# A hybrid pooling and mLSTM layer on one core: where the first phase's transposes, weight casts and modulation stand

## The chip, the core and the metric

The kernel runs on one NeuronCore of a Trainium2 chip. Time is device time in microseconds (us) of one launch, as the median of several runs; lower is better. The engines are named as in the profile: PE (TensorE, matrix products), PEld (PE's weight loads), DVE (VectorE), ACT (ScalarE), POOL (GpSimd) and SP (SyncE, which issues most DMAs).

## What is computed

One layer of a diffusion backbone over 512 latent tokens and 256 context tokens with 1024 channels: modulated RMSNorm, one input projection, a pooling mixer and a bidirectional mLSTM, an output projection, then a modulated RMSNorm and a SwiGLU feed-forward part. Cut to what the change touches:

```python
mod = silu(c) @ w_ada + b_ada              # the same for c_ctx
sh1, sc1, g1, sh2, sc2, g2 = split(mod, 6)
a_lat = rmsnorm(x, norm_mix) * (1 + sc1) + sh1
a_ctx = rmsnorm(ctx, norm_mix) * (1 + csc1) + csh1
p_lat = a_lat @ w_in                       # IN_COLS = 7 * 1024 + 16
p_ctx = a_ctx @ w_in
```

## The kernel before

All products run in float32 on PE with operands that are split in two: `h` is the operand rounded to a shorter format (an ACT cast) and `l` is what is left (a DVE subtraction); a product is then the sum of three, `h*h`, `h*l` and `l*h`. Activations are stored with channels on the 128 partitions, so x is eight blocks (k = 0 to 7) of 128 channels by 512 tokens.

The **first phase** (L352 to L399, about the first 61 us) computes the modulation `sh1, sc1`, the normalised and modulated activations `aT[k]`, and at the same time six column tiles of the input projection (`FIRST`), each accumulated over k in a PSUM bank of its own (`acc0`). Its loop runs over k. The order of PE, ACT and DVE is written out by hand in this phase (`manual_schedule`, L263 to L400): each of these engines takes its instructions in the order in which the code issues them. Behind L400 a scheduler orders them, and it may put instructions of later code between those of the phase. SP's order is the scheduler's too. What belongs to block k:

- `mod_rows(k)` (L272): a DMA of 1 MB of w_ada (`ada`, three buffers), eight small products (L279) into a PSUM bank, and an ACT copy of the result into SBUF (L282).
- `mod_cols(k)` (L285): two PE transposes of that copy (L288) turn rows into columns; three small DVE operations (L290, L292, L293) make from them the shift `shm[k]` and the scale `sm[k]`.
- `stage(k)` (L334): a DMA of six weight tiles (`wr`, three buffers), their cast on ACT (L339, `wh`, two buffers), and through `modulate` (L295) the activation: DVE multiplies x by scale and by the norm's factor (L299), ACT adds the shift and casts (L300, the `h` half `a`), DVE computes the weights' `l` half (L341, `wl`, two buffers), and DVE the activation's `l` half (L303).
- `products(k)` (L344): 18 matmuls (L347), six banks by three halves, in the order `(wh, ah)`, `(wh, al)`, `(wl, ah)` in each bank.

Before the loop, blocks 0 and 1 are staged. The loop's step k issues the first nine products of k, `mod_rows(k + 2)`, the other nine products, then `mod_cols(k + 2)` and `stage(k + 2)`. So block k + 2 is ready one whole step before it is used. Further work hangs on some of the steps: in steps 0 to 3 two squares and their sums for the context's norm (L220 to L227), at the end of step 4 and step 5 the norm's factor of the context (PE products L237 and L253, DVE L243, an ACT copy L395), at the end of steps 5 and 6 `ctx_quad` (L313), which modulates four blocks of the context each (four DVE operations L325, four of ACT L327, four of DVE L329), and in step 6 the load of the weights for the values (L154, L157, L158). After the phase PE goes on to the values' products (L578 to L580).

Two instructions of later code matter below. `crow_setup` (L424) loads the conditioning row `crow_s`, takes its tanh on ACT (L96, into `pb`) and combines the two on DVE (L100). They have no place of their own in the hand-written order.

Of the kernel before, what the change touches and what calls it, by code (L numbers as in the profile page):

```python
# [10 lines left out]
F32 = mybir.dt.float32  # L11
F32R = mybir.dt.float32r
# [7 lines left out]
KT = D // P  # L20
# [30 lines left out]
def layer_kernel(ctx: ExitStack, tc, xT, cT, w0, w1, wv0, wv, wada_a, wada_b, par, crow, bg, wpool,  # L51
                 wout, wffi, wffo, icnt, consts, out):
    nc = tc.nc
    V = nc.vector
# [16 lines left out]
    def tl(tag, shape, dtype=F32, bufs=1, align=None):  # L71
        cnt[0] += 1
        return homes[tag].tile(shape, dtype, name=f"{tag}_{cnt[0]}", tag=tag, bufs=bufs, align_bytes=align)

    def S(tag, dtype=F32):
        return tl(tag, [P, T], dtype, BUFS[tag], HALFLINE if tag in shifted else LINE)
# [4 lines left out]
    def PS(tag="ps"):  # L81
        cnt[0] += 1
        return ps.tile([P, 512], F32, name=f"{tag}{cnt[0]}", tag=tag, bufs=4)
# [7 lines left out]
    def small(shape, nm, dtype=F32, home="small"):  # L91
        return homes[home].tile(shape, dtype, name=nm, tag=nm, bufs=1)
# [13 lines left out]
    def pcol(base, j):  # L106
        return parm[:, base + j:base + j + 1]
# [21 lines left out]
    x_sb = []  # L129
# [69 lines left out]
    def vload(src, n, i):  # L199

        _, wh, wl = wload(src[:, i * 4 * n:(i + 1) * 4 * n], 4 * n, skip=min(NEXT, WMAX - 4 * n))
        return [(wh[:, c * n:(c + 1) * n], wl[:, c * n:(c + 1) * n]) for c in range(4)]
# [63 lines left out]
    rs_x = S("m")  # L266

    mods = small([P, 48], "mods")
    sm = small([P, KT, 2], "sm")
    shm = small([P, KT, 2], "shm")  # L270

    def mod_rows(k):  # L272

        raw = tl("ada", [P, KT, 256], F32, 3)
        nc.sync.dma_start(raw.rearrange("p k c -> p (k c)"), wada_a[k])
        acc = PS()
        for r in range(2):
            for g in range(4):
                nc.tensor.matmul(acc[32 * g:32 * g + 32, :256], sil[:, 4 * r + g, :], raw[:, 4 * r + g, :],  # L279
                                 start=r == 0, stop=r == 1, tile_position=(0, 32 * g))  # L280
        rows = S("tmp")
        nc.scalar.copy(rows[:, :256], acc[:, :256])  # L282
        return rows

    def mod_cols(k, rows):  # L285
        bank = PS()
        for w in range(2):
            nc.tensor.transpose(bank[:, w * P:(w + 1) * P], rows[:, w * P:(w + 1) * P], ident)  # L288
        both = tl("rc2", [P, 2, 2], F32, 2)
        V.tensor_reduce(both, bank[:, :2 * P].rearrange("p (w g j) -> p w j g", w=2, g=4)[:, :, 0:2, :],  # L290
                        mybir.AxisListType.X, ALU.add)
        V.tensor_scalar(shm[:, k, :], both[:, 0, :], pcol(C_BA, k), None, ALU.add)  # L292
        V.tensor_scalar(sm[:, k, :], both[:, 1, :], bsc1[:, k:k + 1], pcol(C_NM, k), ALU.add, ALU.mult)  # L293

    def modulate(src, r, scale, shift, h, l, between=None):  # L295

        t1 = S("tmp")
        t1 = t1[:, :src.shape[-1]]
        V.scalar_tensor_tensor(t1, src, scale, r, ALU.mult, ALU.mult)  # L299
        nc.scalar.activation(h, t1, AF.Identity, bias=shift)  # L300
        if between:
            between()
        V.scalar_tensor_tensor(l, t1, shift, h.bitcast(F32), ALU.add, ALU.subtract)  # L303
        return h, l

    aT, acT = [], []
# [6 lines left out]
    def ctx_quad(k):  # L313

        if k == 0:
            tl("before_ac", [P, NEXT], F32, 1, HALFLINE)
        t, h, l = [], [], []
        for e in range(4):
            if e % 2 == 0:
                tt, hh, ll = S("tmp"), S("ac", F32R), S("ac", F32R)  # L320
            o = e % 2 * TC
            t.append(tt[:, o:o + TC])
            acT.append((hh[:, o:o + TC], ll[:, o:o + TC]))
        for e in range(4):
            V.scalar_tensor_tensor(t[e], c_sb[k + e], sm[:, k + e, 1:2], rs_c[:, :TC], ALU.mult, ALU.mult)  # L325
        for e in range(4):
            nc.scalar.activation(acT[k + e][0], t[e], AF.Identity, bias=shm[:, k + e, 1:2])  # L327
        for e in range(4):
            V.scalar_tensor_tensor(acT[k + e][1], t[e], shm[:, k + e, 1:2], acT[k + e][0].bitcast(F32),  # L329
                                   ALU.add, ALU.subtract)  # L330

    w_first = []

    def stage(k, r):  # L334

        n = len(FIRST) * P
        raw, wh, wl = tl("wr", [P, WMAX], F32, 3), tl("wh", [P, WMAX], F32R, 2, LINE), tl("wl", [P, WMAX], F32R, 2, LINE)
        nc.sync.dma_start(raw[:, :n], w0[k])
        nc.scalar.copy(wh[:, :n], raw[:, :n])  # L339
        aT.append(modulate(x_sb[k], r, sm[:, k, 0:1], shm[:, k, 0:1], S("a", F32R), S("a", F32R),  # L340
                           lambda: V.tensor_sub(wl[:, :n], raw[:, :n], wh[:, :n].bitcast(F32))))  # L341
        w_first.append([(wh[:, i * P:(i + 1) * P], wl[:, i * P:(i + 1) * P]) for i in range(len(FIRST))])

    def products(k, lo, hi, parts=((0, 0), (0, 1), (1, 0))):  # L344
        for i in range(lo, hi):
            for w, x in parts:
                nc.tensor.matmul(acc0[i], w_first[k][i][w], aT[k][x], start=k + w + x == 0, stop=k == KT - 1 and w == 1)  # L347
# [12 lines left out]
    for t, q in enumerate((sq[0], sq[KT - 1])):  # L360
# [3 lines left out]
        if t == 0:  # L364
            keep_warm(WARM[1], warm)
    sd = stx.power(bank, T // P)
    rows = mod_rows(0)
    keep_warm(WARM[2], warm)
    mod_cols(0, rows)
    r = stx.rstd_rows(sd, ALL)  # L370
    stage(0, r)
    keep_warm(WARM[3], warm)
    rows = mod_rows(1)
    keep_warm(WARM[4], warm)
    products(0, 0, nf, ((0, 0),))
    mod_cols(1, rows)
    nc.scalar.copy(rs_x, r)
    stage(1, rs_x)
    for k in range(KT):
        parts = ((0, 0), (0, 1), (1, 0))[0 if k else 1:]  # L380
        products(k, 0, nf // 2, parts)
        if k + 2 < KT:
            rows = mod_rows(k + 2)
        products(k, nf // 2, nf, parts)
        if k + 2 < KT:
            mod_cols(k + 2, rows)
            stage(k + 2, rs_x)
        if k < 4:
            nc.sync.dma_start(cxt[k], cT[:, k * 512:(k + 1) * 512])
            for e in range(2):  # L390
                stc.add(c_sb[2 * k + e], slice(0, TC))
        if k == 4:
            sd = stc.rstd_cols(slice(0, TC))
        if k == 5:
            nc.scalar.copy(rs_c[:, :TC], stc.rstd_rows(sd, slice(0, TC)))  # L395
        if k == KT - 2:
            wv_first = vload(wv0, DH + NG, 0)
        if k in (5, 6):
            ctx_quad(4 * (k - 5))  # L399
# [129 lines left out]
    late = iter(range(16, 48))  # L529
# [596 lines left out]
    r = st1.rstd_rows(sd, HALF[0])  # L1126
# [13 lines left out]
    class Half:  # L1140
# [26 lines left out]
        def low(self):  # L1167
            V.tensor_sub(self.dst[1][:, self.c], self.s[:, self.c], self.dst[0][:, self.c].bitcast(F32))

    with tc.manual_schedule(engines={mybir.EngineType.PE, mybir.EngineType.Activation, mybir.EngineType.DVE}):  # L1170
# [5 lines left out]
        r = st1.rstd_rows(sd, HALF[1])  # L1176
# [233 lines left out]
```

## Time and profile before

| | |
|---|---|
| median of 3 runs | 887.27 us (884.91 to 887.32) |
| the profiled execution's own time | 886.11 us |
| its span, first to last instruction | 884.3 us |
| PE busy | 874.4 us, 99% |
| DVE busy | 614.7 us, 70% |
| ACT busy | 436.7 us, 49% |
| mean granted clock of PE | 0.998 |

The profile is one execution. A row of the timeline reads: start in us, length in us, engine, line of the kernel, operation, what is written and read, shapes, how often, and in brackets the idle time before it and who ended it. Neighbouring matmuls overlap in the rows (a row is longer than the step to the next one), so PE's pace is read from the starts.

### The profile page before, as it was taken

The page shows a single profiled execution, that of the slowest core. Times are in us where ns is not written, and L with a number is a line of the kernel's source. Part 1 is how long each engine was busy: PE and PEld are TensorE (multiplying, and loading weights), DVE is VectorE, ACT ScalarE, POOL GpSimd, SP SyncE. Part 2 cuts the span into 40 slices and gives each one's busy share as a digit, 9 for nine tenths or more (in the row PEclk, how much of TensorE's full clock was granted, in tenths as well). Part 3 has the DMA queues.
Part 4 walks back from the last instruction along what each step waited for, and adds up shares of the span by engine and source line. Part 5 has one row for each costly group of instructions (what it writes and reads, how often), then busy time and mean ns, then how long its engine had stood idle before and what let it go on. Part 6 is the DMA issues. An engine that isn't in the chain of part 4 may idle for free.

```text
span 884.3 us, 15057 instructions
## 1 busy us (share of the span) xinstructions
PE 874.4 (99%) x5920; PEld 797.7 (90%) x5920; DVE 614.7 (70%) x1187; ACT 436.7 (49%) x823; POOL 66.7 (8%) x93
## 2 busy tenths in 40 slices
PE   9999999999999999999999999999999999999997
PEld 7689798899888998889988899999889998899996
DVE  4678677877876787767886767795366753867644
ACT  4464354455344453444455446673255741666542
POOL 0000010020000100000000000120011100111000
PEclk9999999999999999999999999999999999999999
DMA  9863021436252542434454830384366643755502
GB/s 349 324 196 113 25 72 57 164 113 180 72 187 88 170 141 84 155 109 135 142 149 125 294 111 1 104 221 107 95 176 147 145 119 87 206 142 125 144 1 96
DMA packets 41446, 120.88 MB, mean 137 GB/s; under 512 B 4480, under 2 KB 8864, under 8 KB 40352
## 3 DMA queue, kind: packets, MB, share of 16 engines
q1 hardware_dynamic: 35904, 109.96, 38.2%
q0 software_dynamic: 5472, 9.96, 6.8%
q8 instruction: 46, 0.75, 0.3%
q14 instruction: 24, 0.20, 0.1%
HBM read 116.22 MB, written 3.69 MB: 136 GB/s over the span
## 4 chain that ended last, share of the span: by engine, by line
PE 96%; DVE 1%; ACT 1%; DMA 1%; issue 0%; DVEq 0%; SPq 0%; ACTq 0%
PE ps L187 14%; PE ps L189 13%; PE ps L188 13%; PE ps L197 8%; PE ps L195 8%; PE ps L194 8%; PE pat L347 3%; PE ps L578 3%; PE ps L579 3%; PE ps L580 3%; PE pat L187 2%; PE pat L189 2%; PE pat L188 2%; PE pat L792 2%; PE pat L793 2%; PE pat L794 2%
## 5 line engine op out<-in xcount | busy, mean ns | idle before, releaser
L157 ACT CAST wh<-wr 128x1024 fp32r<-128x1024 f32 (+3 forms) x78 | 78.9, 1011 | 102.7 <-PE ps L188 45.6
L158 DVE TENSOR_TENSOR wl<-wr,wh 128x1024 fp32r<-128x1024 f32 (+3 forms) x78 | 92.6, 1188 | 35.9 <-ACT wh L157 23.8
L194 PE MATMUL ps<-a,wh 128*128 128x512 f32 x272 | 106.5, 392 | 0.0
L195 PE MATMUL ps<-a,wh 128*128 128x512 f32 x272 | 106.3, 391 | 0.0
L187 PE MATMUL ps<-act,wh 128*128 128x512 f32 (+1 forms) x199 | 69.2, 348 | 0.0
L188 PE MATMUL ps<-act,wh 128*128 128x512 f32 (+1 forms) x199 | 69.0, 347 | 0.0
L189 PE MATMUL ps<-act,wl 128*128 128x512 f32 (+1 forms) x199 | 69.0, 347 | 0.0
L197 PE MATMUL ps<-a,wl 128*128 128x512 f32 x272 | 68.0, 390 | 0.0
L195 PEld LDWEIGHTS ps<-a,wh 128*128 128x128 f32 x272 | 51.1, 188 | 10.2
L194 PEld LDWEIGHTS ps<-a,wh 128*128 128x128 f32 x272 | 51.1, 188 | 10.2
L197 PEld LDWEIGHTS ps<-a,wl 128*128 128x128 f32 x272 | 50.8, 188 | 10.5
L1030 POOL DMA_DIRECT2D ol<-in_wffi x38 | 33.4, 897 | 254.7 <-ACT ol L1029 124.4
L187 PE MATMUL ps<-hp,gh 128*128 128x256 f32 x176 | 49.9, 284 | 0.4 <-ACT gh L176 0.4
L189 PE MATMUL ps<-hp,ol 128*128 128x256 f32 x176 | 48.8, 277 | 0.5 <-DVE ol L1027 0.5
L188 PE MATMUL ps<-hp,gh 128*128 128x256 f32 x176 | 49.0, 278 | 0.0
L1251 DVE SCALAR_TENSOR_TENSOR x<-ps,lb,x 128x512 f32<-128x512 f32 (+1 forms) x32 | 19.6, 616 | 42.1 <-PE ps L189 42.1
L189 PE MATMUL ps<-hp,gl 128*128 128x256 f32 x176 | 48.9, 278 | 0.0
L187 PE MATMUL ps<-hp,oh 128*128 128x256 f32 x176 | 48.8, 277 | 0.0
L188 PE MATMUL ps<-hp,oh 128*128 128x256 f32 x176 | 48.7, 277 | 0.0
L537 DVE SCALAR_TENSOR_TENSOR pb<-pb,crow_s 128x1024 f32<-128x1024 f32 x32 | 38.9, 1233 | 10.1 <-DMA pb<-in_wada_b 10.1
L187 PEld LDWEIGHTS ps<-act,wh 128*128 128x128 f32 x199 | 37.5, 188 | 4.8
L188 PEld LDWEIGHTS ps<-act,wh 128*128 128x128 f32 x199 | 37.5, 188 | 4.8
(365 smaller groups left out, 2726.4 us busy)
## 6 DMA issues: line engine op xcount, KB each, us to landing
wr<-in_w SPq DMA_DIRECT2D x42, 512.0 KB, 3.5
pb<-in_wada_b SPq DMA_DIRECT2D x32, 512.0 KB, 4.2
wr<-in_wffi SPq DMA_DIRECT2D x25, 512.0 KB, 4.3
ur<-in_wffi SPq DMA_DIRECT2D x19, 512.0 KB, 4.0
ol<-in_wffi POOLq DMA_DIRECT2D x38, 256.0 KB, 4.9
ada<-in_wada_a SPq DMA_DIRECT2D x8, 1024.0 KB, 9.8
wr<-in_wffo SPq DMA_DIRECT2D x16, 448.0 KB, 3.6
wr<-in_wout SPq DMA_DIRECT2D x8, 512.0 KB, 3.5
```

What stands on the lines that cost most here:

```text
L157: nc.scalar.copy(wh, raw[:, :n])
L158: V.tensor_sub(wl, raw[:, :n], wh.bitcast(F32))
L187: nc.tensor.matmul(dst, wh, ah, start=first and i == 0, stop=False, skip_group_check=on)
L188: nc.tensor.matmul(dst, wh, al, start=False, stop=False, skip_group_check=on)
L189: nc.tensor.matmul(dst, wl, ah, start=False, stop=last and i == n - 1, skip_group_check=on)
L194: nc.tensor.matmul(dst, wh, ah, start=first and i == 0, stop=False)
L195: nc.tensor.matmul(dst, wh, al, start=False, stop=False)
L197: nc.tensor.matmul(dst, wl, ah, start=False, stop=last and i == len(wparts) - 1)
L347: nc.tensor.matmul(acc0[i], w_first[k][i][w], aT[k][x], start=k + w + x == 0, stop=k == KT - 1 and w == 1)
L537: V.scalar_tensor_tensor(wa[:, :D], wa[:, :D], 0.5, crow_s, ALU.mult, ALU.mult, accum_out=mods[:, i:i + 1])
L578: nc.tensor.matmul(acc[:, :n], ah, wh, start=kk == 0, stop=False)
L1030: nc.gpsimd.dma_start(l, dram, accum_op=ALU.add)
```

## The change

`stage` is cut in two: `first_weights(k)` (DMA, cast, and the weights' `l` half) and `modulated(k)` (the activation). `mod_rows` can leave its ACT copy to a later call of `mod_copy`. Blocks 0 and 1, staged before the loop, are as before. In the loop:

```diff
-    def stage(k, r):
+    def first_weights(k, sub=True):
...
+    def modulated(k, r, between=None):
+        aT.append(modulate(x_sb[k], r, sm[:, k, 0:1], shm[:, k, 0:1], S("a", F32R), S("a", F32R), between))
+
+    def stage(k, r):
+        modulated(k, r, first_weights(k, False))
...
     for k in range(KT):
         parts = ((0, 0), (0, 1), (1, 0))[0 if k else 1:]
+        ahead = 0 < k < KT - 1
+        if ahead:
+            first_weights(k + 1)
         products(k, 0, nf // 2, parts)
+        if ahead:
+            mod_cols(k + 1, rows)
         if k + 2 < KT:
-            rows = mod_rows(k + 2)
+            acc = mod_rows(k + 2, True)
+        if ahead:
+            modulated(k + 1, rs_x)
+        if k + 2 < KT:
+            rows = mod_copy(acc)
         products(k, nf // 2, nf, parts)
-        if k + 2 < KT:
-            mod_cols(k + 2, rows)
-            stage(k + 2, rs_x)
         if k < 4:
```

The transposes and the modulation of a block thus move from the end of the step two before its use into the middle of the step just before its use. The arithmetic is the same. Lines behind the change are numbered 13 to 19 higher (the products L347 become L360, the transposes L288 become L291, the context's L325, L327 and L329 become L328, L330 and L332).

On PE, in step 3, the rows before show the modulation's products for block 5 between two groups of nine products, and the transposes for the same block at the end of the step (`a` and `wh`, `wl` are the operands of step 3; the last row is the first of step 4):

```order
L347 MATMUL pat_150<-a_367,wl_364 128x512
L279 MATMUL ps_449<-ada_447,sil 32x256 x8
L347 MATMUL pat_151<-a_367,wh_363 128x512
...
L347 MATMUL pat_109<-a_367,wl_364 128x512
L288 MATMUL ps_469<-ident,tmp_458 128x128 x2
L347 MATMUL ps_148<-a_424,wh_420 128x512
```

In the changed kernel the same place on PE reads:

```order
L360 MATMUL pat_150<-a_395,wl_364 128x512
L291 MATMUL ps_434<-ident,tmp_401 128x128 x2
L279 MATMUL ps_443<-ada_441,sil 32x256 x8
L360 MATMUL pat_151<-a_395,wh_363 128x512
...
L360 MATMUL pat_109<-a_395,wl_364 128x512
```

The transposes, now those of block 4, stand directly ahead of the modulation's products, and nothing stands between the last product of a step and the first of the next, except L237 and L253 at the ends of steps 4 and 5.

On DVE, at the end of step 5, the rows before are the last of block 7 (`rc_119` and `a_595`), then the context's `ctx_quad`, then the row of `crow_setup`:

```order
L290 TENSOR_REDUCE rc_119_585<-ps_582 128x4
L292 TENSOR_SCALAR shm<-rc_119_585,parm 128x2
L293 TENSOR_SCALAR sm<-rc_119_585,bsc_89,parm 128x2
L299 SCALAR_TENSOR_TENSOR tmp_596<-x_103,sm,m_144 128x512
L341 TENSOR_TENSOR wl_591<-wr_589,wh_590 128x768
L303 SCALAR_TENSOR_TENSOR a_595<-tmp_596,shm,a_594 128x512
L325 SCALAR_TENSOR_TENSOR tmp_606<-cx_153,sm,m_157 128x256 x2
L325 SCALAR_TENSOR_TENSOR tmp_609<-cx_154,sm,m_157 128x256 x2
L329 SCALAR_TENSOR_TENSOR ac_608<-tmp_606,shm,ac_607 128x256 x2
L329 SCALAR_TENSOR_TENSOR ac_611<-tmp_609,shm,ac_610 128x256 x2
L100 SCALAR_TENSOR_TENSOR crow_s<-pb_706,crow_s 128x1024
```

In the changed kernel the same work on DVE (`a_566` is the last of block 6; `wl_607`, `rc_130` and `a_628` belong to block 7) reads:

```order
L306 SCALAR_TENSOR_TENSOR a_566<-tmp_567,shm,a_565 128x512
L328 SCALAR_TENSOR_TENSOR tmp_587<-cx_153,sm,m_157 128x256 x2
L328 SCALAR_TENSOR_TENSOR tmp_590<-cx_154,sm,m_157 128x256 x2
L332 SCALAR_TENSOR_TENSOR ac_589<-tmp_587,shm,ac_588 128x256 x2
L332 SCALAR_TENSOR_TENSOR ac_592<-tmp_590,shm,ac_591 128x256 x2
L346 TENSOR_TENSOR wl_607<-wr_605,wh_606 128x768
L293 TENSOR_REDUCE rc_130_623<-ps_620 128x4
L100 SCALAR_TENSOR_TENSOR crow_s<-pb_706,crow_s 128x1024
L295 TENSOR_SCALAR shm<-rc_130_623,parm 128x2
L296 TENSOR_SCALAR sm<-rc_130_623,bsc_89,parm 128x2
L302 SCALAR_TENSOR_TENSOR tmp_629<-x_103,sm,m_144 128x512
L306 SCALAR_TENSOR_TENSOR a_628<-tmp_629,shm,a_627 128x512
```

All of block 7 now stands behind the context's eight operations, and the row of `crow_setup` stands inside it. On ACT the same piece before, from the copy of block 7's modulation rows (`tmp_571`) on:

```order
L282 COPY tmp_571<-ps_562 128x256
L339 CAST wh_590<-wr_589 128x768
L96 ACTIVATE pb_706<-crow_s 128x1024
L300 ACTIVATE a_594<-tmp_596,shm 128x512
L395 COPY m_157<-ps_601 128x256
L327 ACTIVATE ac_607<-tmp_606,shm 128x256 x2
L327 ACTIVATE ac_610<-tmp_609,shm 128x256 x2
L157 CAST wh_644<-wr_642 128x1088
```

and in the changed kernel:

```order
L285 COPY tmp_571<-ps_556 128x256
L414 COPY m_157<-ps_582 128x256
L330 ACTIVATE ac_588<-tmp_587,shm 128x256 x2
L330 ACTIVATE ac_591<-tmp_590,shm 128x256 x2
L342 CAST wh_606<-wr_605 128x768
L96 ACTIVATE pb_706<-crow_s 128x1024
L303 ACTIVATE a_627<-tmp_629,shm 128x512
L157 CAST wh_644<-wr_642 128x1088
```

On ACT, too, the cast of block 7's weights and its activation now follow the context's four operations. On SP the context's loads (`cx`) now stand one place ahead of the weights' loads (`wr`) in the first steps, and the load of `crow_s` stands behind the second load for the values (L154) and not ahead of it. POOL's order is the same.

More of the change, by code (lines that the diff above doesn't have):

```diff
@@ L270, in layer_kernel, with mod_rows @@
     shm = small([P, KT, 2], "shm")
-    def mod_rows(k):
+    def mod_rows(k, late=False):
         raw = tl("ada", [P, KT, 256], F32, 3)
@@ L280, in mod_rows, with mod_copy @@
                                  start=r == 0, stop=r == 1, tile_position=(0, 32 * g))
+        return acc if late else mod_copy(acc)
+    def mod_copy(acc):
         rows = S("tmp")
@@ L339, in stage, with low @@
         nc.scalar.copy(wh[:, :n], raw[:, :n])
-        aT.append(modulate(x_sb[k], r, sm[:, k, 0:1], shm[:, k, 0:1], S("a", F32R), S("a", F32R),
-                           lambda: V.tensor_sub(wl[:, :n], raw[:, :n], wh[:, :n].bitcast(F32))))
         w_first.append([(wh[:, i * P:(i + 1) * P], wl[:, i * P:(i + 1) * P]) for i in range(len(FIRST))])
+        def low():
+            V.tensor_sub(wl[:, :n], raw[:, :n], wh[:, :n].bitcast(F32))
+        if sub:
+            low()
+        return low
+    def modulated(k, r, between=None):
+        aT.append(modulate(x_sb[k], r, sm[:, k, 0:1], shm[:, k, 0:1], S("a", F32R), S("a", F32R), between))
+    def stage(k, r):
+        modulated(k, r, first_weights(k, False))
     def products(k, lo, hi, parts=((0, 0), (0, 1), (1, 0))):
```

## The prediction, as it was put on record

> **What bounds the kernel now.** I read the page first, then the waits of PE over the whole run, then the timelines of PE, DVE and ACT for the first 61 us, where the change acts. The page's chain of waits, by engine:
>
> ```profile
> span 884.3 us, 15057 instructions
> PE 96%; DVE 1%; ACT 1%; DMA 1%; issue 0%; DVEq 0%; SPq 0%; ACTq 0%
> ```
>
> The path to the end is PE. The waits of PE in the whole run (line waited for, total us, times, longest):
>
> ```profile
> PE ps L189 <- DVE ol L1027: 0.5, 1, 0.5
> PE pat L752 <- ACT tmp L803: 0.4, 1, 0.4
> PE pat L189 <- DMA ol<-in_wffi: 0.4, 1, 0.4
> PE ps L187 <- ACT gh L176: 0.4, 1, 0.4
> PE pat L666 <- DVE g_nM L664: 0.2, 1, 0.2
> ```
>
> Behind the start PE waits for others 1.9 us in all, none of it in the first phase. PE takes its matmuls in order, so a microsecond that PE loses at 57 us has almost nothing later in which to vanish: at most these 1.9. The change can act in two ways: by what PE itself does in a step, and by making PE wait where it doesn't now.
>
> **What a step costs PE.** Step 2 to step 3 on PE (starts, then lengths; the steps between starts count):
>
> ```profile
> 31.45 0.39 PE L347 MATMUL pat<-a,wl 128*128 128x512 f32 x1
> 31.77 1.07 PE L279 MATMUL ps<-ada,sil 128*32 128x256 f32 x16
> ...
> 34.74 0.40 PE L347 MATMUL pat<-a,wl 128*128 128x512 f32 x1
> 34.98 0.38 PE L288 MATMUL ps<-ident,tmp 128*128 128x128 f32 x2
> 35.12 0.71 PE L347 MATMUL ps<-a,wh 128*128 128x512 f32 x2
> 35.66 0.40 PE L347 MATMUL ps<-a,wl 128*128 128x512 f32 x1
> ```
>
> and the ends of steps 4 and 5, the start of step 7, and the first values' product behind it:
>
> ```profile
> 46.14 0.38 PE L288 MATMUL ps<-ident,tmp 128*128 128x128 f32 x2
> 46.36 0.51 PE L237 MATMUL ps<-ones,tmp 128*128 128x2 f32 x4
> 46.72 0.71 PE L347 MATMUL ps<-a,wh 128*128 128x512 f32 x2
> ...
> 52.18 0.38 PE L288 MATMUL ps<-ident,tmp 128*128 128x128 f32 x2
> 52.40 0.61 PE L253 MATMUL ps<-ident,rc 128*128 128x128 f32 x4
> 52.76 0.71 PE L347 MATMUL ps<-a,wh 128*128 128x512 f32 x2
> ...
> 56.96 0.61 PE L347 MATMUL ps<-a,wh 128*128 128x512 f32 x2
> ...
> 61.04 0.28 PE L578 MATMUL ps<-wh,a 128*128 128x272 f32 x1
> ```
>
> The 18 products of step 7, with nothing between them, take 61.04 - 56.96 = 4.08 us, 0.227 each. Against that pace three borders cost extra. (i) From a product to the modulation's products: 31.77 - 31.45 = 0.32, so 0.09 extra. (ii) From transposes back to products: two products in 35.66 - 35.12 = 0.54 and not 0.455, so 0.09 extra. (iii) From transposes to other small products: 46.36 - 46.14 = 0.22, where transposes ahead of products take 35.12 - 34.98 = 0.14, so 0.08 extra.
>
> **The change on PE.** Each loop step with modulation products had borders (i) and (ii); now it has (iii) in their place. Counted up to the first product of step 6: (ii) falls away four times (starts of steps 1 to 4), (i) five times but comes back twice (products now stand directly ahead of L237 and L253), (iii) comes five times and goes twice, and one pair of transposes, block 7's, has moved behind this point. That is -4 x 0.09 - 3 x 0.09 + 3 x 0.08 - 0.14 = -0.53 us: L253 would start at 52.40 - 0.53 = 51.87 and step 6 at 52.23. The changed order's border is not in the trace at this place; L237's row is the nearest. Ends: only the transposes' 0.14, or 0.8 if (iii) costs nothing. Block 7's transposes come back in step 6 with 0.14 + 0.09, so PE alone would win 0.3 us by step 7, which would start at 56.96 - 0.53 + 0.23 = 56.66.
>
> **The wait in steps 1 to 5.** The modulation chain was a step ahead; now it must end between the middle of a step and its end. Its measured lengths, on DVE for block 5, with ACT's part:
>
> ```profile
> 35.40 0.17 DVE L290 TENSOR_REDUCE rc<-ps 128x4 f32<-128x16 f32 x1 [1.77 <-PE ps L288]
> ...
> 36.06 0.75 DVE L299 SCALAR_TENSOR_TENSOR tmp<-x,sm,m 128x512 f32<-128x512 f32 x1
> 36.73 0.95 DVE L341 TENSOR_TENSOR wl<-wr,wh 128x768 fp32r<-128x768 f32 x1
> 37.61 0.75 DVE L303 SCALAR_TENSOR_TENSOR a<-tmp,shm,a 128x512 fp32r<-128x512 f32 x1
> ```
>
> ```profile
> 34.94 0.83 ACT L339 CAST wh<-wr 128x768 fp32r<-128x768 f32 x1 [1.61 <-PE pat L347]
> 36.85 0.72 ACT L300 ACTIVATE a<-tmp,shm 128x512 fp32r<-128x512 f32 x1 [1.07 <-DVE tmp L299]
> ```
>
> Transposes start at 34.98; reduce +0.42; L299 +0.66; ACT's half +0.79; DVE's half +0.76 and 0.75 long: 3.38 us, plus 0.04 of handover (ACT ends at 37.57, DVE starts at 37.61). PE takes from the transposes to the second product of the next step, the first that reads the `l` half: 0.22, then 34.98 - 31.77 = 3.21 from the modulation's products to the step's end, then 0.23: 3.66 us. It fits with 0.24 to spare. The cast starts where it did, since it waited and waits for PE to free `wh` (the bracket of its row), so cast and subtraction, 0.83 and 0.95, are done before the transposes, 2 us into the step. The context's squares and sums stand behind the chain and ahead of the next cast, covered by the same 2 us. The queue of SP has the context's loads ahead of the weights' now; the weights have a step in hand. I cost these steps' waits at nothing; with the cover gone they cost five times what exceeds 0.24.
>
> **The wait ahead of step 7.** Here the context's block stands in between. Its rows on DVE and ACT:
>
> ```profile
> 55.48 1.67 DVE L325 SCALAR_TENSOR_TENSOR tmp<-cx,sm,m 128x256 f32<-128x256 f32 x4
> 57.07 1.67 DVE L329 SCALAR_TENSOR_TENSOR ac<-tmp,shm,ac 128x256 fp32r<-128x256 f32 x4
> 58.65 1.23 DVE L100 SCALAR_TENSOR_TENSOR crow_s<-pb,crow_s 128x1024 f32<-128x1024 f32 x1
> 59.78 1.30 DVE L158 TENSOR_TENSOR wl<-wr,wh 128x1088 fp32r<-128x1088 f32 x1
> ```
>
> ```profile
> 52.92 1.06 ACT L96 ACTIVATE pb<-crow_s 128x1024 f32<-128x1024 f32 x1
> ...
> 54.68 0.35 ACT L395 COPY m<-ps 128x256 f32<-128x256 f32 x1
> ...
> 56.00 1.72 ACT L327 ACTIVATE ac<-tmp,shm 128x256 fp32r<-128x256 f32 x4 [0.96 <-DVE tmp L325]
> 57.62 1.09 ACT L157 CAST wh<-wr 128x1088 fp32r<-128x1088 f32 x1
> ```
>
> In the order before, block 7 was finished on DVE ahead of L325 (the first row starts at 55.48), and PE needed it at 56.96; the context's eight operations delayed nobody. Now they stand ahead of block 7, and cannot start until L253 has run:
>
> - L253 from 51.87, 0.61 long; copy on ACT 0.35, two handovers of 0.04: DVE's four start at 52.91.
> - Four by 57.07 - 55.48 = 1.59, four by 58.65 - 57.07 = 1.58: DVE free at 56.08. ACT meanwhile starts its four 0.52 later than DVE's, takes 57.62 - 56.00 = 1.62 and then casts block 7's weights in 0.83: done at 55.88, in time.
> - The weights' subtraction, 37.61 - 36.73 = 0.88: 56.96.
> - Reduce to L299 takes 0.66, and `crow_s` between them 59.78 - 58.65 = 1.13: 58.75. Its tanh on ACT (1.06 behind the cast) is ready by 56.95, just in time.
> - ACT's half at +0.79, 59.54; DVE's half at +0.76, 60.30, 0.75 long, handover 0.04: 61.09.
>
> PE's second product of step 7 waits for that; by PE's own pace it would come at 56.66 + 0.23 = 56.89. So PE stands **4.2 us**. The other 16 and itself follow at 17 x 0.227 = 3.86: the values' products start at 64.95 in place of 61.04, **3.9 us later**. The 0.3 us won is in that sum. Queued behind the waiting product on PE is the rest of the kernel. The values' weights (cast on ACT and L158 on DVE, 1.1 and 1.3 us) come behind block 7, while PE still has 3.86 us of step 7: hidden.
>
> Two loads stand behind this. `crow_s` now follows the second values' load:
>
> ```profile
> 48.87 0.33 SPq L154 DMA_DIRECT2D wr<-in_wv  x1
> crow_s<-in_crow SPq DMA_DIRECT2D x1, 512.0 KB, 4.7
> ```
>
> Issued 0.4 us behind that load, or earlier, it lands at 54 at the latest, ahead of its tanh at 55.8.
>
> Bounds: with the gain up to L253 between 0.14 and 0.8 (0.53 taken) the shift is 4.3 or 3.6; a dozen handovers read to 0.05 add 0.4 either way: +3.2 to +4.7.
>
> **Clock while PE stands.** In slices of the first microseconds (PE busy and its count of matmuls after the slice's length; the clock column reads 1.00) PE starts slowly:
>
> ```profile
> 4.00:5.00 1.00, 1.00 (x7) 1.00 (x7) 0.00 (x0) 0.00 (x0) 0.00 (x0) 1.00 1.07 397
> 7.00:8.00 1.00, 1.00 (x11) 1.00 (x10) 0.69 (x1) 0.90 (x3) 0.00 (x0) 1.00 1.02 414
> ```
>
> The same warm-up matmuls come at 7 per us and later at 11, the change lying near 6 us, some 5 us after PE's first. If PE fell back to that pace after its wait, 5 us of it would cost 5 x (1 - 7/11) = 1.8 us. The wait here would be 3.5 us without any matmul, then one product, then 0.6 more. [...] No wait of this length follows the start in this trace, so it cannot show it; by the row alone I leave the sum at 3.9.
>
> **From the profile to the time.** The profiled execution took 886.11 us; plus 3.9 it would take 890.0. It lay 1.2 below the median of the runs; on the median, 887.27 + 3.9 = **891.2 us**.
>
> **Rivals.**
> - Clock: the pace drops after the wait, 887.27 + 5.7 = 893.0. For it: the slow start. [...] 0.14.
> - Tight steps: the chain's 0.24 in steps 1 to 5 is not there, say 0.3 short of it each time: 3.9 + 5 x 0.3, 892.7. Against: every length in it is measured in the same surroundings. 0.07.
> - Lost time comes back: the delay gives DVE, ACT and DMA a lead that removes PE's five later waits, 1.9 us: 889.3. Against: four of the five are fed by PE's own results. 0.08.
> - Other side: block 7 isn't held up, because DVE reaches it ahead of the context's operations; then PE keeps its 0.3, 887.0. It decides at 56.9: the chain must end 4.2 us earlier than I sum it, which is the context's eight operations and `crow_s` together (1.59 + 1.58 + 1.13 = 4.3). The order shows these ahead of it on the same engine. 0.05.
>
> My forecast keeps 0.66. A measurement of this kernel can tell about 0.3%, 2.7 us, from no change: slower means above 889.9. The forecast lies 1.3 above that, with 0.8 of its own bounds and runs that spread by 2.4; I give it 0.86 on that side: 0.57, with the two dearer rivals 0.78. Same: the rest of the forecast and the cheaper rivals, 0.19; faster 0.03. The range leaves out the other side, part of the returned time and the ends of the dearer cases: 888.8 to 893.8.
>
> **What would show it.** In the profile after: L253 near 51.9; L328 directly behind its copy; L346 of block 7 near 56; a wait of PE at L360 for ACT's half and then DVE's half (L303, L306) of 3 to 4 us in all between 56 and 61.5; the values' products (L597) near 65; no other new wait. A wait of PE in steps 1 to 5, or a step 7 whose products come at less than the 0.227 pace, would be the rivals. Wrong I would be if step 7 starts before 58 us.

## The result, and the profile after

| | before | after |
|---|---|---|
| median of 6 runs each, side by side | 886.12 us (884.91 to 887.32) | 892.61 us (891.62 to 893.9) |
| the profiled execution's own time | 886.11 us | 893.9 us |
| its span | 884.3 us | 892.1 us |
| mean granted clock of PE | 0.998 | 0.994 |

The ratio is 1.0077, 95% interval [1.0067, 1.0087]: slower by 6.5 us. The forecast was 891.2, 3.9 us more than before. The time lies in the range, the sign is right, and 2.6 us of the loss are not in the sum. The profiled execution of after is the slowest of its six (7.8 us above before's), so the size of the loss is taken from the medians.

The chain of waits by engine, and the waits of PE (line waited for, total us, times, longest):

```profile
span 892.1 us, 15054 instructions
PE 94%; DVE 3%; DMA 1%; ACT 1%; issue 0%; DVEq 0%; SPq 0%; POOL 0%; POOLq 0%
```

```profile
PE ps L360 <- ACT a L303: 3.5, 2, 3.4
PE pat L143 <- DVE warm L114: 1.4, 1, 1.4
PE ps L187 <- ACT pm L176: 1.0, 1, 1.0
```

The first three rows of the waits are shown. The first is new: the products of the first phase wait for ACT's half of an activation. Twice, but 0.15 us of it lies at 17.72; the 3.4 are one wait. PE's timeline around it, up to the first product of the values:

```profile
56.16 0.39 PE L360 MATMUL pat<-a,wl 128*128 128x512 f32 x1
59.91 1.58 PE L360 MATMUL ps<-a,wh 128*128 128x512 f32 x2 [3.35 <-ACT a L303]
61.29 0.63 PE L360 MATMUL ps<-a,wl 128*128 128x512 f32 x1
61.72 1.05 PE L360 MATMUL ps<-a,wh 128*128 128x512 f32 x2
62.57 0.63 PE L360 MATMUL ps<-a,wl 128*128 128x512 f32 x1
...
66.06 0.39 PE L360 MATMUL pat<-a,wl 128*128 128x512 f32 x1
66.29 0.63 PE L360 MATMUL pat<-a,wh 128*128 128x512 f32 x2
66.75 0.40 PE L360 MATMUL pat<-a,wl 128*128 128x512 f32 x1
66.99 0.29 PE L597 MATMUL ps<-wh,a 128*128 128x272 f32 x1
```

Two things are to be seen. The product that starts at 56.16 is the last one until 59.91: the wait of the prediction. And behind it a group of three products takes 62.57 - 61.29 = 1.28 us, 0.43 each, where the last three take 66.75 - 66.06 = 0.69, 0.23 each: PE runs at half its pace until 65.6. The slices of after say so in their clock column (the number ahead of the last two):

```profile
56.00:59.90 3.90, 0.55 (x3) 0.13 (x1) 3.08 (x7) 1.32 (x3) 0.23 (x3) 0.86 0.45 142
59.90:65.60 5.70, 5.69 (x13) 4.13 (x14) 4.02 (x8) 2.63 (x5) 0.00 (x0) 0.50 0.71 203
65.60:66.90 1.30, 1.30 (x7) 1.08 (x6) 1.30 (x4) 1.11 (x3) 0.00 (x0) 0.98 0.71 204
```

If the clock is either full or half, as the two paces say, 0.86 over 3.9 us means 2 x 0.14 x 3.9 = 1.1 us at half, then 5.7, then 0.05: 6.8 us together.

Why PE waits stands on DVE and ACT:

```profile
52.63 1.68 DVE L328 SCALAR_TENSOR_TENSOR tmp<-cx,sm,m 128x256 f32<-128x256 f32 x4 [1.16 <-ACT m L414]
54.23 1.67 DVE L332 SCALAR_TENSOR_TENSOR ac<-tmp,shm,ac 128x256 fp32r<-128x256 f32 x4
55.81 0.96 DVE L346 TENSOR_TENSOR wl<-wr,wh 128x768 fp32r<-128x768 f32 x1
56.67 0.17 DVE L293 TENSOR_REDUCE rc<-ps 128x4 f32<-128x16 f32 x1
56.76 1.22 DVE L100 SCALAR_TENSOR_TENSOR crow_s<-pb,crow_s 128x1024 f32<-128x1024 f32 x1
...
58.35 0.75 DVE L302 SCALAR_TENSOR_TENSOR tmp<-x,sm,m 128x512 f32<-128x512 f32 x1
59.89 0.75 DVE L306 SCALAR_TENSOR_TENSOR a<-tmp,shm,a 128x512 fp32r<-128x512 f32 x1 [0.79 <-ACT a L303]
```

```profile
54.77 0.82 ACT L342 CAST wh<-wr 128x768 fp32r<-128x768 f32 x1
55.50 1.06 ACT L96 ACTIVATE pb<-crow_s 128x1024 f32<-128x1024 f32 x1
59.13 0.72 ACT L303 ACTIVATE a<-tmp,shm 128x512 fp32r<-128x512 f32 x1 [2.58 <-DVE tmp L302]
```

Block 7 stands behind the context's eight operations and has `crow_s` in its middle, without a gap from 52.63 on except for ACT's half. That is the prediction's chain.

Executions differ by up to 1 us before the modulation even begins (its first products start between 12.66 us, e6, and 13.65, e2), so I measure the phase from the first of the modulation's products to the first of the values' products. The first modulation's row of before and of after:

```profile
13.63 1.07 PE L279 MATMUL ps<-ada,sil 128*32 128x256 f32 x16
```

```profile
13.22 1.07 PE L279 MATMUL ps<-ada,sil 128*32 128x256 f32 x16
```

Before 61.04 - 13.63 = 47.41 us, after 66.99 - 13.22 = 53.77: **+6.36**. Of the 7.8 us by which this execution is longer, that is the larger part; what stands behind the phase took 892.1 - 66.99 = 825.1 us and not 884.3 - 61.04 = 823.3, another 1.8 us. It loses them between 470 and 485 us, where DVE stood 2.46 us for a load of `icnt`, and PE behind it 1.0 and 0.2. So the phase and the medians' 6.5 agree only to within the microsecond or two that single executions gain or lose elsewhere.

```profile
471.04 0.69 DVE L512 TENSOR_TENSOR tmp<-pb,tmp 128x512 f32<-128x512 f32 x1 [2.46 <-DMA tmp<-in_icnt]
```

Before's profile has no such wait. It turns up in e6, 2.74 us long, whose median is that of before all the same, and 1.07 us long in e4, whose blocks 2 to 6 go by the old order. Whether the change makes it likelier is not shown.

### The profile page after: what moved, and what is told of

It reads as the page before. It is cut to its first block, busy times and chain, and to the rows that moved or that the text cites. A ratio compares the mean times of both kernels' runs of the same rounds, so it can differ in the third digit from the quotient of the medians.

```text
span 892.1 us, 15054 instructions
## 1 busy us (share of the span) xinstructions
PE 877.1 (98%) x5920; PEld 799.3 (90%) x5920; DVE 615.4 (69%) x1187; ACT 436.7 (49%) x823; POOL 66.7 (7%) x93
## 4 chain that ended last, share of the span: by engine, by line
PE 94%; DVE 3%; DMA 1%; ACT 1%; issue 0%; DVEq 0%; SPq 0%; POOL 0%; POOLq 0%
PE ps L187 14%; PE ps L188 13%; PE ps L189 13%; PE ps L197 8%; PE ps L195 7%; PE ps L194 7%; PE ps L597 3%; PE ps L598 3%; PE ps L599 3%; PE pat L360 2%; PE pat L187 2%; PE pat L188 2%; PE pat L189 2%; PE pat L811 2%; PE pat L813 2%; PE pat L812 2%
## 5 line engine op out<-in xcount | busy, mean ns | idle before, releaser
L189 PEld LDWEIGHTS ps<-act,wl 128*128 128x128 f32 x199 | 37.5, 188 | 4.8
L188 PEld LDWEIGHTS ps<-act,wh 128*128 128x128 f32 x199 | 37.5, 189 | 4.8
```

The source lines that it names most:

```text
L188: nc.tensor.matmul(dst, wh, al, start=False, stop=False, skip_group_check=on)
L189: nc.tensor.matmul(dst, wl, ah, start=False, stop=last and i == n - 1, skip_group_check=on)
```

## The experiments

Theory A: PE's wait ahead of step 7 makes the loss, and it comes from what stands ahead of block 7 on DVE (the context, `crow_s`); a stretch at half pace comes on top. Rivals: the slow pace costs nothing that a later stage wouldn't lose anyway; the new order costs by itself, in steps 1 to 5 or through later loads. In the table "phase" is the length just defined less that of before, "clock" is PEclk from step 7's first product to the values' first, both of one profiled execution each; "time" is the median less that of before on the same chip.

| kernel | wait ahead of step 7, us | clock | phase | time | ratio |
|---|---|---|---|---|---|
| after | 3.35, then a part not listed | 0.60 | +6.36 | +6.5 | 1.0077 [1.0067, 1.0087] |
| e11, after again | 3.35 + 0.28 | 0.73 | +5.68 | +5.9 | 1.0069 [1.0056, 1.0082] |
| e12, `crow_s` alone moved | 2.35 + 0.29 | 0.73 | +4.67 | +4.1 | 1.0047 [1.0035, 1.006] |
| e5, half the context ahead | 3.0 + 0.3 | 0.73 | +5.28 | +4.8 | 1.0054 [1.0042, 1.0067] |
| e4, order alone | 1.5 + 0.3 | 0.73 | +3.95 | +3.3 | 1.0037 [1.0025, 1.005] |
| e2, context behind | 2.59 + 0.28 | 1.00 | +3.28 | +4.8 | 1.0058 [1.0045, 1.0071] |
| e7, context and `crow_s` behind | 0.21 + 0.29 | 1.00 | +0.91 | +3.0 | 1.0034 [1.0022, 1.0047] |
| e1, block 7 as before | 0.32 | 1.00 | +0.43 | +2.1 | 1.0021 [1.0012, 1.003] |
| e6, block 7 and `crow_s` as before | none | 1.00 | -0.19 | -0.3 | 1.0 [0.9992, 1.0009] |
| e3, 32 matmuls in the wait | none | 1.00 | +7.00 | +6.3 | 1.007 [1.0056, 1.0084] |
| e3b, 16 matmuls in the wait | 0.28 | 1.00 | +4.04 | +7.3 | 1.0084 [1.007, 1.0098] |
| e3c, the same again | 0.29 | 1.00 | +4.05 | +6.4 | 1.0071 [1.0057, 1.0085] |
| e10, 16 matmuls in before | none | 1.00 | +3.59 | +4.7 | 1.0051 [1.0039, 1.0064] |

**e1: block 7 by the old order.** Blocks 2 to 6 by the new one.

```diff
-        ahead = 0 < k < KT - 1
+        ahead = 0 < k < KT - 2
...
+        if k == KT - 3:
+            mod_cols(k + 2, rows)
+            stage(k + 2, rs_x)
```

> The changed order for blocks 2 to 6; block 7 is transposed, cast and modulated at the end of step 5, ahead of the context's block, as in the kernel before. Theory A (the loss is block 7 standing behind the context's eight operations and crow_s, plus the slow pace that follows PE's wait): no wait of PE at step 7, granted clock as before (0.998), step 7's products at 0.227 us, and time 0.3 us below the kernel before, from 0 to 0.8 below; not to be told from it. Rival B (the loss comes from the tighter modulation chain or the moved transposes and casts of all steps): most of the 6.5 us stay, at least +3.

Measured 888.3 us. The wait and the slow stretch are gone, so it is block 7's place that makes them; but 2.1 us remain, which no theory had. Step 7's second product still waits, for block 7's last number:

```profile
PE ps L360 <- DVE a L306: 0.3, 1, 0.3
```

```profile
54.28 1.06 ACT L96 ACTIVATE pb<-crow_s 128x1024 f32<-128x1024 f32 x1 [1.60 <-DMA crow_s<-in_crow]
```

```profile
55.37 1.23 DVE L100 SCALAR_TENSOR_TENSOR crow_s<-pb,crow_s 128x1024 f32<-128x1024 f32 x1 [0.83 <-ACT pb L96]
56.51 0.74 DVE L306 SCALAR_TENSOR_TENSOR a<-tmp,shm,a 128x512 fp32r<-128x512 f32 x1
```

ACT stands 1.6 us for the load of `crow_s`, which the change had put behind the second values' load, and block 7's last number stands behind that. e6 takes this away.

**e4: the order alone.** In the kernel before, the context's block is issued ahead of block 7's, and nothing else is changed.

```diff
-        if k + 2 < KT:
+        if k + 2 < KT - 1:
             mod_cols(k + 2, rows)
             stage(k + 2, rs_x)
...
+        if k == 5:
+            ctx_quad(0)
+            mod_cols(k + 2, rows)
+            stage(k + 2, rs_x)
```

> The kernel before with one thing moved: the context's first four blocks are issued ahead of block 7's transposes and stage at the end of step 5; all other steps are as before. Theory A: PE waits ahead of step 7. From L253 at 52.4, its 0.6, the copy 0.35, 1.59 and 1.58 for the context, 0.66 + 0.79 + 0.76 + 0.75 for block 7 the second product comes at 59.65 in place of 57.2: 2.5 us later, of them about 1.5 without a matmul, which is too short for the slow pace: time +2.5 (2 to 3), clock 0.998. Rival B (the loss comes from the transposes and casts moved in all steps): no change, within 1 us.

Measured 889.48 us: the order alone makes a wait of 1.5 + 0.3 us and a loss of 3.3 (2.2 to 4.4), where 2 to 3 were expected. The profiled execution also has a slow stretch, for which I had held the wait to be too short, though no run had shown that:

```profile
PE ps L347 <- ACT a L300: 1.5, 1, 1.5
...
PE ps L347 <- DVE a L303: 0.3, 1, 0.3
```

```profile
59.50:64.50 5.00, 5.00 (x16) 3.94 (x15) 4.78 (x11) 2.79 (x6) 0.00 (x0) 0.66 0.80 265
```

A clock of 0.66 over 5 us is 2 x 0.34 x 5 = 3.4 us at half. This execution is the slowest of the five, 891.12 us at a mean clock of 0.996; the four others took 888.44 to 889.5 us at 0.997 to 0.998 and may have had no such stretch, so the median doesn't show its price.

**e5: half of the context ahead of block 7.**

```diff
-        if k in (5, 6):
-            ctx_quad(4 * (k - 5))
+        if k == 5:
+            ctx_quad(0, 2)
+        if k == 6:
+            ctx_quad(2, 2, False)
+            ctx_quad(4)
```

> The changed kernel with two of the context's first four blocks issued behind block 7. The chain ahead of block 7 is shorter by half of 1.59 and of 1.58, 1.6 us, so PE stands 1.8 us without a matmul in place of 3.4. Theory A with a clock that only falls after a wait of some 3 us: the values' products start at about 63.0 (2.4 later than before), products of step 7 at 0.227, clock 0.998, time +2.4 (2 to 3). Rival (any wait of PE of this kind brings the slow pace): time +4.5 or more and a lower clock.

Measured 890.93 us, and a miss: the wait shrank by less than 0.4, so the run doesn't say what a wait of 1.8 us does. That the clock only falls behind some 3 us no run shows, and e4 speaks against it: 0.66 over 5 us behind 1.5 + 0.3. The rows of e5 show the second gate behind the first one; with less context in front, ACT waits for `crow_s` to land:

```profile
55.26 1.06 ACT L96 ACTIVATE pb<-crow_s 128x1024 f32<-128x1024 f32 x1 [0.49 <-DMA crow_s<-in_crow]
```

**e2 and e7: all of the context behind block 7, then `crow_s` too.**

```diff
-        if k in (5, 6):
-            ctx_quad(4 * (k - 5))
+        if k == 6:
+            ctx_quad(0)
+            ctx_quad(4)
```

In e7, `crow_setup()` stands between the two calls, and its load ahead of the second values' load.

> The changed kernel with both halves of the context's modulation issued behind block 7's modulation, crow_s's pair still ahead of it. Theory A: VectorE no longer has 3.35 us of context in front of block 7, crow_s's 1.22 us stay; TensorE waits about 1.9 us ahead of step 7 in all (0.9 for the chain of block 7 itself, since step 6 has no modulation products that would cover it, and 1.0 for crow_s); the wait is over 1.5 us, so 3.4 us at half pace follow, worth about 1.6; values' products start +3.0 against before, 889.2 us (888.4 to 890). Without the slow stretch: +1.5, 887.7. Rival (the context's lateness then holds the values' products, since they read it): +3 with a full clock and the wait at the values' products.

> As the run before it, and crow_s's pair is put by hand between the two halves of the context, its load ahead of the second values' load as in the kernel before. Theory A: only block 7's own chain is left ahead of step 7, from the transposes at 54.1 to about 57.5: TensorE waits about 0.9 us, no slow stretch, values' products at +0.6 to +0.9 if the context is ready by then: 886.9 us (886.3 to 887.6). Rival (the context, now last, holds the values' products): +1.5 to +2.5, with a wait for VectorE's or ScalarE's context numbers there.

e2 took 890.79 us, above the 888.4 to 890 expected. Its wait was 2.6 + 0.3 and not 1.9, since `crow_s` again came late:

```profile
55.11 1.06 ACT L96 ACTIVATE pb<-crow_s 128x1024 f32<-128x1024 f32 x1 [1.35 <-DMA crow_s<-in_crow]
```

The profiled execution of e2 is its fastest run, 889.25 us at a mean clock of 0.998, with a clock of 1.00 in step 7:

```profile
59.50:64.30 4.80, 4.45 (x18) 3.48 (x19) 4.52 (x9) 3.40 (x8) 0.00 (x0) 1.00 0.43 150
```

The four others were granted 0.996 to 0.997 and took 890.76 to 893.37. One stretch of 3.4 us at half is 1.7 / 889 = 0.2% of the mean clock: that fits a stretch of some 1.5 us that comes in some executions and not in others. It is no proof, since before's executions lie at 0.997 to 0.999 without such a stretch: the mean also counts some microseconds at half behind the last product (in before the 4.0 us from 880.3 on).

e7 took 888.97 us. The wait ahead of step 7 is 0.5 us, where 0.9 was expected, but the rival came true, and dearer than I had priced it (+3.0 and not +1.5 to +2.5): the context, now last, holds what comes behind.

```profile
67.65 0.39 PE L599 MATMUL ps<-wh,a 128*128 128x272 f32 x1 [0.68 <-ACT tmp L96]
75.51 0.36 PE L599 MATMUL ps<-wh,ac 128*128 128x272 f32 x1 [0.43 <-DVE gif L608]
```

So the context can't simply go behind block 7 in this order: step 6 has no modulation's products, and only half of that step lies between block 7's transposes and its use.

**e12: `crow_s` alone.** The changed kernel, with `crow_s` loaded ahead of the second values' load and its pair issued between the context's halves.

```diff
         if k == KT - 2:
             wv_first = vload(wv0, DH + NG, 0)
+            nc.sync.dma_start(crow_s, crow.broadcast_to([P, D]))
+            crow_setup()
...
-    crow_setup()
```

> The changed kernel with only crow_s moved: its load ahead of the second values' load, its pair between the two halves of the context and so behind block 7. Theory A: of the chain to block 7's last number 1.2 us of VectorE go (56.76 to 57.95 in the changed kernel), the first product of step 7 goes out near 58.7 in place of 59.9, TensorE waits 2.9 us in all instead of 4.2; with 3.4 us at half pace behind that the time is 1.2 to 2.5 under the changed kernel: 890.7 us (889.9 to 891.5). Rival (crow_s was covered, the order of the context alone sets the wait): 892.6.

Measured 890.11 us, 1.8 under the changed kernel beside it (e11), as expected. Block 7's chain without `crow_s` in it:

```profile
56.47 0.17 DVE L293 TENSOR_REDUCE rc<-ps 128x4 f32<-128x16 f32 x1
56.68 0.23 DVE L295 TENSOR_SCALAR shm<-rc,parm 128x2 f32<-128x2 f32 x1
...
57.13 0.75 DVE L302 SCALAR_TENSOR_TENSOR tmp<-x,sm,m 128x512 f32<-128x512 f32 x1
```

```profile
58.69 0.49 PE L360 MATMUL ps<-a,wh 128*128 128x512 f32 x1 [2.35 <-ACT a L303]
59.48 0.62 PE L360 MATMUL ps<-a,wh 128*128 128x512 f32 x1 [0.29 <-DVE a L306]
```

From the reduction to L302 it takes 0.66 in place of 1.68, and PE's wait is a microsecond shorter. The phase is 1.0 us shorter than in e11; the rest of the 1.8 lies outside it. The profiled execution of e11 lost 1.2 us at the load of `icnt` and that of e12 nothing.

**e6: block 7 and `crow_s` as before, blocks 2 to 6 by the change.** e1's edit and e12's together; it differs from e12 in block 7's order alone.

> The kernel in which blocks 2 to 6 go by the new order and block 7 by the old, with crow_s's load put ahead of the second values' load and its pair behind the context's first half, both as in the kernel before. Theory A (what that kernel lost came from crow_s's load, which had moved behind the second values' load, and its pair, which then stood ahead of block 7's last number): nothing is left but what TensorE saves in steps 2 to 6, 0.06 us each: 885.9 us (885.4 to 886.4), ratio 0.9997. Rival (the new order of steps 2 to 6 itself costs, through something later that the first phase's DMAs set): 887.5 to 888.3 as without the two moves.

Measured 885.7 us, ratio 1.0 [0.9992, 1.0009]: no difference from before. The whole loss is thus undone by two moves, 890.11 - 885.70 = 4.4 us (on two chips, whose kernels before differ by 0.04) by block 7's place and 1.8 by `crow_s`: 6.2 of 5.9 to 6.5. The change's reordering of blocks 2 to 6 costs nothing and gains 0.19 in the phase, less than a measurement can tell. e1's 2.1 us go with the moves of `crow_s`, though e1's profiled execution, 886.98 us and one of its three fastest, shows only 0.43 + 0.19 of them in the phase; where the rest lay isn't shown. e6 is the fastest version found, and it doesn't beat before.

**e3, e3b, e3c, e10: the wait covered.** To keep the clock up, PE multiplies a constant tile into an unused bank ahead of step 7: 32 times in e3, 16 in e3b and e3c. e10 has the same 16 in the kernel before, where PE doesn't wait.

```diff
+        if k == KT - 1:
+            idle = PS()
+            for i in range(16):
+                nc.tensor.matmul(idle[:, :P], warm, warm, start=True, stop=True)
```

> The changed kernel with 32 small products of a zero tile, about 0.1 us each, put on PE ahead of step 7's, into a free bank: PE works while it waits for block 7, the wait itself is left as it is. It adds 32 products that nothing reads. Theory A with the clock as a second term: the granted clock stays at 0.998, step 7's products come 0.227 us apart, the values' products start about 3.9 us later than in the kernel before, and the time is 3.9 to 4.6 us above it, some 2 to 2.5 below the changed kernel. Rival C (the slow pace of step 7 has nothing to do with PE standing idle, for instance it comes from the operands or from traffic): products 0.42 us apart as in the changed kernel and time 6 us or more above the kernel before.

> The changed kernel with 16 matmuls of the constant tile into an unused bank ahead of step 7's products. In the run with 32 such pairs one took 0.22 us and all 7.06 us, longer than the wait of 4.2 us; 16 should take 3.5 us and end at about 60.3, when block 7's numbers are ready anyway. Theory A (the wait, then a slower TensorE): the products of step 7 run 0.227 us apart, the values' products start near 64.5 in place of 66.99, granted clock 0.998, the time 886.2+3.7 = 889.9 us (889.2 to 890.6), some 2.5 us less than the changed kernel. Rival (the slow pace is not worth time, since the next stage would wait anyway): 892 or more, as the changed kernel. Rival B (the matmuls cost what the clock gives back): between the two, 891.

> The changed kernel itself, beside the next two on one chip, for a second profiled execution of it. Theory A: TensorE waits 4.2 us ahead of step 7 again, one or two stretches of 3.4 us at half pace follow, 892.6 us (891.6 to 893.5).

> The kernel with 16 matmuls of the constant tile ahead of step 7 once more, beside the changed kernel on the same chip, since its first run put the values' products 2.5 us earlier than the changed kernel and yet ended no earlier. If those 2.5 us count and the first time was made by the rest of the program, it is 1.5 to 2.5 us under the changed kernel beside it. If they don't count, it is within 0.7 us of it again; then the profile shows where after 60 us they are lost.

> The kernel before with the same 16 matmuls of the constant tile ahead of step 7, where TensorE waits for nothing: what they cost by themselves. 16 pairs of 0.11 us are 3.5 us: 889.6 us (889.2 to 890.2), and the values' products 3.5 us later. If such matmuls cost more later in the program than where they stand, as the first run with them suggests, it is 891 or more with the values' products no later than that.

e3 took 892.45 us, but its matmuls cost twice what I had put them at, 0.22 us each, so that they ran 3 us past the wait; its time can't tell what the cover is worth. e3b, with the right number, started the values' products as early as expected and yet took 893.26 us, so I ran it again (e3c: 892.4) beside the changed kernel (e11: 891.92) and beside its matmuls alone (e10: 890.67, between the two cases expected). At their place the three covers do what theory A says: the same operands and loads, but no slow pace (a clock of 1.00 in all three, 0.60 in after, 0.73 in e11), so it is PE's standing idle that brings it. In e3c:

```profile
56.35 3.73 PE L400 MATMUL ps<-warm 128*128 128x128 f32 x32
59.86 0.49 PE L360 MATMUL ps<-a,wh 128*128 128x512 f32 x1
60.65 0.50 PE L360 MATMUL ps<-a,wh 128*128 128x512 f32 x1 [0.29 <-DVE a L306]
```

```profile
59.80:64.50 4.70, 4.41 (x21) 3.44 (x20) 4.42 (x9) 3.30 (x8) 0.00 (x0) 1.00 0.55 178
```

Block 7 is ready when it was in after, the clock stays at 1.00, and the phase is 6.36 - 4.05 = 2.3 us shorter than in after, 1.6 than in e11. In the time nothing of it is left. Part of that is lost much later, near the end, and e10 loses it too, though it never waited. PE's matmuls between 800 and 850 us in before, e10, and e3c (the number behind PE's busy time):

```profile
800.00:850.00 50.00, 50.00 (x438) 50.00 (x438) 33.11 (x55) 28.86 (x56) 4.36 (x5) 1.00 0.43 108
```

```profile
800.00:850.00 50.00, 49.40 (x426) 49.20 (x426) 31.50 (x53) 28.11 (x53) 4.38 (x5) 1.00 0.48 117
```

```profile
800.00:850.00 50.00, 48.97 (x420) 48.56 (x419) 32.10 (x54) 27.73 (x53) 5.25 (x6) 1.00 0.47 120
```

At 50 / 438 us a matmul the 12 missing ones are 1.4 us and the 18 are 2.1; after, e11, e12 and e3 have 434, 437, 438 and 439 there. PE stands for a late cast of weights in that stretch, 0.6 us in e10 and 1.0 in e3c; e10's longest wait, 1.3 us for a load of the feed-forward's, lies elsewhere, at 574 us. Counted from the same matmul, the one that before starts at 811 us, up to the last one of the program, e10 takes 2.2 us longer than before, e3c 1.8 and e3b 1.2. But e4, e5 and e7, which have no such matmuls, take 1.1 to 1.6 us longer there too, and all other kernels 0.1 at most, e3 with twice as many matmuls among them. So the added matmuls as such don't make this loss, and what does isn't known. Nor is the cover the only difference: after and e11 lost 1.8 and 1.2 us at the load of `icnt`, where e3c lost nothing. So this is open: that the half pace lengthens the phase by 1.6 to 2.4 us is shown, that removing it shortens the whole program is not.

## Why the prediction was right or wrong

- **What PE itself does in a step**: right in sign, too large. Predicted gain up to L253 0.53; from the first modulation's product to L253 it is 52.40 - 13.63 = 38.77 before and 51.59 - 13.22 = 38.37 after, 0.40. Two borders were not as read:

```profile
31.00 0.38 PE L291 MATMUL ps<-ident,tmp 128*128 128x128 f32 x2
31.31 1.07 PE L279 MATMUL ps<-ada,sil 128*32 128x256 f32 x16
...
45.33 0.39 PE L360 MATMUL pat<-a,wl 128*128 128x512 f32 x1
45.56 0.50 PE L237 MATMUL ps<-ones,tmp 128*128 128x2 f32 x4
...
51.36 0.39 PE L360 MATMUL pat<-a,wl 128*128 128x512 f32 x1
51.59 0.61 PE L253 MATMUL ps<-ident,rc 128*128 128x128 f32 x4
```

Transposes ahead of the modulation's products take 0.31 and not the 0.22 that I read off at L237, and from a product to L237 or L253 it takes 0.23, with nothing extra: that border belongs to the modulation's products, not to small products as such.

- **No wait in steps 1 to 5**: right. PE's list has none there above 0.15 us, and e6, which keeps this order in blocks 2 to 6, costs nothing. The rival of the tight steps didn't come.
- **The wait ahead of step 7**: right. Predicted L253 at 51.87, L346 at 56.08, the chain's end at 61.09, a wait of 4.2. Found 51.59, 55.81, and L306 from 59.89 on, 0.75 long: 60.64, which with 0.04 of handover is 60.68. At its own pace the second product would have come at 56.16 + 2 x 0.227 = 56.61: the wait is 60.68 - 56.61 = 4.07. That the context's eight operations and `crow_s` are what makes it is shown by e12 and e6, which take them away. That `crow_s` would land in time was right for after, whose tanh doesn't wait for it; it was near, as e1, e2 and e5 show.
- **The pace behind the wait**: wrong, and this is the step that failed: "by the row alone I leave the sum at 3.9", which puts the clock behind the wait at nothing. From 60.68 the other seventeen at 0.227 would end at 64.54; they ended at 66.99, 2.45 us later. So -0.16 from PE's own steps (56.16 + 0.23 - 13.22 against 56.96 - 13.63), + 4.07, + 2.45 make the 6.36. The rival Clock, given 0.14, is what happened in the phase, with 2.4 where it had 1.8: I had priced it at 5 us of 7/11, and it was 4.9 us of one half. Its 5.7 was the 3.9 and the 1.8 worked out from the slow start; that no wait of this length follows the start in the trace before was no ground to leave the 1.8 out. The length of the wait alone doesn't decide it: behind 1.5 + 0.3 us the clock was 0.66 over 5.0 us (e4), behind 2.59 + 0.28 it was 1.00 over 4.8 in the one profiled execution of e2. The stretches at half pace, worked out from the mean clocks, are 3.4 us in e4, 2 x 0.34 x 5.0 = 3.4 in e11, 2 x 0.27 x 6.4 = 3.5 in e12, 2 x 0.28 x 6.2 = 3.5 in e5 and 6.8 in after.
- **When the clock falls**, which the prediction left open, the traces show in part. In after, in slices of 0.02 us, it goes from 1.00 to 0.50 at 58.82, 58.82 - 56.55 = 2.27 us behind the end of PE's last product (56.16 + 0.39), and back to 1.00 at 65.65, 6.83 us later, though PE has had products again from 59.91 on. In six profiled executions PE stood 1.5 us or more ahead of step 7. Five of them have a slow stretch (after, e4, e5, e11, e12); e2 has none, though its 2.59 + 0.28 us are more than e4's 1.5 + 0.3 and e12's 2.35 + 0.29. What decides between them is not shown, and no run was made to test it.
- **From the sum to the time**: helped by the base. The three runs before had a median of 887.27; in all later comparisons it is 885.98 to 886.18. On a base of 886.1 the same sum gives 890.0, 2.6 us short; the number on record stood 1.2 us nearer than its sum deserved, and that is luck. The 2.45 us of the slow pace are about what is missing, but since the cover of e3c took them out of the phase and nothing out of the time, that they fill it is not shown.
- **Lost time comes back, the other side**: neither came. PE's later waits in after are not fewer.

## What to carry to other kernels

When work is moved nearer to its use, sum the chain on the engine that computes it in the new order, with everything that the order now puts in front, the operations included that have no place of their own (here `crow_s`), and compare it with what the waiting engine has left to do; the wait that it gave held to 0.1 us. Then add the clock: here a wait of 1.5 us or more was followed by about 3.4 us, or twice that, at half pace in five of six profiled executions, and the stretch differed between two executions of one program (6.8 us in after, 3.4 in e11). So a wait like these should be priced as a wait plus 0 to 2.4 us, not left out because the trace before doesn't show it. And an operation that only gained a later load (the `crow_s` row here) is the next gate as soon as the first one is removed.

## What the runs showed of the hardware

- PE's clock went to half (0.50 in after's slices) behind waits of 1.5 to 3.4 us: for about 3.4 us by the mean clock in e4 (wait 1.5 + 0.3), e12 (2.35 + 0.29), e5 (3.0 + 0.3) and e11 (3.35 + 0.28), for 6.8 us in after (3.35, then a part not listed). So of two executions of one program, after and e11, one had 6.8 us and the other 3.4. A wait of 2.59 + 0.28 us left the clock at 1.00 (e2).
- A float32 matmul of 128 x 128 by 128 columns took 0.22 us in a row of 32 (e3) or 16 (e3c, (59.86 - 56.35) / 16; two passes each in the rows), about as much as one product of step 7 with 512 columns, whose operands are in the shorter format (0.227).
- The 3.5 us of matmuls that were put into before (e10) cost 4.7 in the time, with an interval of 3.5 to 5.7. Its profiled execution lost 2.2 us in the last stage, as e4, e5 and e7 lost 1.1 to 1.6 there, for a reason that stays open.
